# A two-layer mixer block on one core: an opening by quarters of the features instead of halves, and a retention that begins one step later in layer 0

## The chip, the cores and the metric

One Trainium2 chip, one of its cores. A core has a matrix engine (PE in the profile, with its weight loads as PEld), a vector engine (DVE), a scalar engine (ACT), GpSimd (POOL) and a queue engine (SP) that issues most transfers. The metric is the device time of one execution in microseconds (us); the kernel before takes 1234.97 us, the median of three runs (1234.73 to 1236.95).

## The reference

Two layers run over a latent stream `x` and a context stream `ctx`, each 256 tokens by 1024 features, in fp32. Cut to what the opening of the kernel computes and what uses it:

```python
for l in range(DEPTH):                                   # DEPTH = 2
    mod_l = silu(c) @ w_mod[l] + b_mod[l]                # 6 * 1024 values for the latent stream
    mod_c = silu(c_ctx) @ w_mod[l] + b_mod[l]            # the same for the context
    sh1, sc1, g1, sh2, sc2, g2 = split(mod_l, 6)         # csh1, csc1, ... from mod_c
    h_lat = rmsnorm(x, norm_g[l, 0]) * (1 + sc1) + sh1
    h_ctx = rmsnorm(ctx, norm_g[l, 0]) * (1 + csc1) + csh1
    p_lat, p_ctx = h_lat @ w_in[l], h_ctx @ w_in[l]      # 9 * 256 columns of q, k, v, ..., then 4 * 1024 of gates
    y_c, s_f, s_b = retention(rope_less(q_c), k_c, v_c)  # both directions, 4 heads of 64
    y_l, _, _ = retention(rope(q_l), rope(k_l), v_l, s_f, s_b)
    merged = sum(sigmoid(gates[i]) * (branch[i] @ w_branch[i]) for i in range(4))
    x = x + g1 * rmsnorm(merged @ w_o[l], norm_g[l, 1])  # branches: retention, conv, Fourier, pool
    x = x + g2 * rmsnorm(swiglu(rmsnorm(x) * (1 + sc2) + sh2), norm_g[l, 3])
    # ctx in the same way, in layer 0 alone
```

## The kernel before

The features are kept transposed: eight chunks of 128 features on the partitions, 512 columns (256 latent tokens, then 256 context tokens). Every fp32 product is made of three matmuls of rounded parts, high by high, high by low and low by high (`mm3`, L206 to L210). Weights come in blocks of 512 KB: `_load` (L95) issues the transfer on SP, `_split` makes the high part on ACT (L103) and the low part on DVE (L113), into a ring of four buffer pairs; raw blocks have two buffers for each tag. The program is one list of steps. A step names the blocks that it needs, and `pump` runs ahead of the steps with loads and splits as far as buffers are free; each engine then works its instructions in the order in which they were written. A DMA on SP that waits for its buffer or its semaphore therefore holds those behind it.

The opening is `begin` (L1313 on), with `clear`, `v_part` and `qk_part` (L1066 to L1100). It loads `x`, normalises it (`x_norm`: squares on ACT L423, a power on POOL L429, the scaling on DVE L1335) and turns it (`x_turn`, L1344). Meanwhile it makes the shift and scale of the modulation: the two conditioning vectors, padded to 32 columns (`cs`), are the stationary operand, and a block of `w_mod` is streamed against them (`mod_mm`, L263). The rows of the result are copied out by ACT (`modrows`, L1367), transposed (`modt`, L279), and added to their biases on DVE (L284 to L286). With them `modulate` makes a chunk of the hidden stream (`hf` L461 and L463, `h0hi` L467, `h0lo` L450). Then V, K and Q of both streams are accumulated in PSUM banks that stay occupied (`vps`, `kps`, `qps`). Those banks are first set to zero by matmuls with a zero operand (L1076, L1080), some of which only keep the engine busy (`WARM`).

It does this by halves of the features. Half 0 (chunks 0 to 3) needs eight blocks of `w_mod`; each block holds one chunk of contraction rows by the shift and scale columns of half of the features, in two matmuls of 512 columns. After them the V, K and Q parts of half 0 (12 matmuls each) alternate with the eight blocks of half 1, and then the parts of half 1 follow. 24 parts of 12 make 288 matmuls of 256 columns. After the last Q part the gate steps begin (`g_step`, `gps`, L208 to L210, 512 columns). The rotary step of K and Q (`rotate`, ACT L722 and L724, DVE L725 to L727) runs beside them, with one buffer (`roper`), and needs the `rope` table, which `fixed` loads on SP. From the first `g_step` a generator `both` advances the retention piece by piece, one at each step (its transposes `ktp` L760, its states `st` L776, its scores, its output `y` L813).

Of the kernel before, what the change touches and what calls it, by code (L numbers as in the profile page):

```python
# [33 lines left out]
MOD_ORDER = (0, 2, 1, 3)  # L34
# [4 lines left out]
WARM = (3,)  # L39
# [22 lines left out]
class Weights:  # L62
# [76 lines left out]

    def split_to(self, nth):  # L140
# [17 lines left out]
def kernel(ctx: ExitStack, tc: tile.TileContext, a: dict, out: bass.AP):  # L158
# [46 lines left out]

    def mm3(ps, st, mv, first, last):  # L206
# [38 lines left out]
    chan = load(cst, [P, DEPTH, 2, 4], a["chan"], "chan", nc.scalar)  # L245
    bsel = load(cst, [P, 2], a["c_bsel"], "bsel", nc.scalar)
    e12 = load(dec, [P, 2, 2 * PIECE], a["c_e12"], "e12", nc.scalar)
    kexp = load(dec, [P, 2, 2], a["c_kexp"], "kexp", nc.scalar)
# [8 lines left out]
    def mod_mm(k, half, raw):  # L257
        if "ps" not in mods:
            mods["ps"] = bank("m", "modps")
        ps = mods["ps"]  # L260
        for j in range(2):
            q = 2 * half + j
            nc.tensor.matmul(  # L263
                ps[32 * q : 32 * q + 32, :],
                lhsT=cs[:, k, :],
                rhs=raw[:, j * 512 : (j + 1) * 512],
                start=(k == 0),
                stop=(k == KC - 1),
            )
# [4 lines left out]
    def mod_cols(half, tiles, rows):  # L274

        pt = bank("b", f"modt{half}", [4, 64])
        hs = slice(64 * half, 64 * half + 64)
        for cb in range(4):
            nc.tensor.transpose(pt[:, cb, :], rows[hs, cb * P : (cb + 1) * P], ident[hs, hs])  # L279
        am, sh = tiles  # L280
        ks = slice(4 * half, 4 * half + 4)
        for s in range(2):
            b = [bcol[:, 0, kind, ks] for kind in range(2)]
            nc.vector.tensor_tensor(sh[:, s, ks], pt[:, :, s], b[0], op=ALU.add)  # L284
            nc.vector.tensor_tensor(am[:, s, ks], pt[:, :, 32 + s], b[1], op=ALU.add)
            nc.vector.scalar_tensor_tensor(  # L286
                am[:, s, ks], am[:, s, ks], 1.0, gcol[:, 0, 0, ks], op0=ALU.add, op1=ALU.mult
            )
# [325 lines left out]
    def mixer(l, h, hnext, start=None):  # L614
# [124 lines left out]
        def both():  # L739
            yield from retention(0)  # L740
# [320 lines left out]
        if l == 0:  # L1061
            vps, kps, qps = {}, {}, {}

            def clear():
# [4 lines left out]
                yield  # L1069
                for i in range(2):  # L1070
                    vps[i], kps[i] = bank("a", f"vps{i}", [2, MIX]), bank("a", f"kps{i}")
                for n in (0, *WARM):
                    for i in range(2):
                        for ps in (vps[i].rearrange("p a b -> p (a b)"), kps[i]):
                            for _ in range(n or 1):
                                nc.tensor.matmul(ps, lhsT=z[:, :P], rhs=z, start=n == 0, stop=False)  # L1076
                    yield
                for i in range(2):
                    qps[i] = bank("b", f"qps{i}", keep=True)
                    nc.tensor.matmul(qps[i], lhsT=z[:, :P], rhs=z, start=True, stop=False)  # L1080
                yield

            def v_part(w, half, t):
                ps, ts = vps[t // 2][:, t % 2, :], slice(t * P, (t + 1) * P)
                for i in range(4):
                    k, sl = 4 * half + i, slice(i * MIX, (i + 1) * MIX)
                    mm3(ps, (h[0][k][:, ts], h[1][k][:, ts]), (w.hi[:, sl], w.lo[:, sl]), False, k == KC - 1 and t % 2 == 1)
                if half and t % 2:
                    for j in range(2):
                        center(vps[t // 2][:, j, :], t - 1 + j)  # L1090

            def qk_part(w, half, isq, c, s):
# [499 lines left out]
```

## Time and profile before

| | us |
|---|---|
| median of three runs | 1234.97 (1234.73 to 1236.95) |
| the profiled execution | 1234.56 |
| its span, first to last instruction | 1232.8 |
| PE busy in it | 1196.1 (97%) |
| DVE, ACT, POOL busy | 783.7 (64%), 452.1 (37%), 41.1 (3%) |
| PE's first matmul starts | 9.13 |
| first V matmul starts | 25.84 |
| first gate matmul starts | 76.37 |

The span is about 1.8 us shorter than the execution's time, which also covers what lies around it; the profiled execution is 0.4 us below the median. A line of the profile names the line of the program, the engine, the operation, the tile written and the tiles read, with start and duration in us. Matmuls are pipelined: the distance of two starts tells what one costs in a row, and its own duration is longer. In square brackets stands how long the engine was idle before an instruction, and what ended that.

### The profile page before, as it was taken

How to read it: one execution, taken by the hardware profiler on the slowest of the kernel's cores; microseconds unless marked ns; L12 is line 12 of the kernel's file. 1: busy time of each engine (PE TensorE's matmuls, PEld its weight loads, DVE VectorE, ACT ScalarE, POOL GpSimd, SP SyncE). 2: the span in 40 equal slices, each digit the busy share in tenths (PEclk: the TensorE clock that was granted, in tenths of full speed). 3: DMA queues.
4: the chain of work that ended last, by engine and by line, in shares of the span. 5: the costliest groups of instructions: out<-in, count | busy, mean ns of one | idle time of the engine just before them, and what ended most of it. 6: DMA issues, size and time to landing. Idle time of an engine off the chain costs nothing.

```text
span 1232.8 us, 17240 instructions
## 1 busy us (share of the span) xinstructions
PE 1196.1 (97%) x6774; PEld 1025.4 (83%) x6774; DVE 783.7 (64%) x1274; ACT 452.1 (37%) x714; POOL 41.1 (3%) x39
## 2 busy tenths in 40 slices
PE   6999999999999989999999999989999999999997
PEld 3687878888888788888888888789889998999986
DVE  4455654477876565776777774476666666666644
ACT  4332332332232443222322222454345445444532
POOL 1500000000000000000000000000000000000000
PEclk9999999999999999999999999999999999999999
DMA  8543424456655234666766773334355563666672
GB/s 302 178 114 94 116 86 156 157 170 144 219 184 187 69 103 140 219 211 141 262 192 201 233 263 92 115 123 144 117 162 185 177 232 123 188 187 185 194 220 86
DMA packets 66435, 205.65 MB, mean 167 GB/s; under 512 B 14641, under 2 KB 18481, under 8 KB 66353
## 3 DMA queue, kind: packets, MB, share of 16 engines
q1 hardware_dynamic: 65200, 204.31, 53.1%
q8 instruction: 53, 0.87, 0.3%
q10 hardware_dynamic: 1152, 0.24, 0.1%
q14 instruction: 30, 0.24, 0.1%
HBM read 203.41 MB, written 1.11 MB: 166 GB/s over the span
## 4 chain that ended last, share of the span: by engine, by line
PE 89%; DVE 4%; ACT 3%; issue 1%; DMA 1%; POOL 0%; SPq 0%; DVEq 0%; POOLq 0%; ACTq 0%
PE up L210 10%; PE up L209 10%; PE up L208 10%; PE gate L208 7%; PE gate L210 7%; PE gate L209 7%; PE dn L210 4%; PE dn L209 4%; PE dn L208 4%; PE pb L208 2%; PE pb L210 2%; PE pb L209 2%; PE wo L210 1%; PE wo L208 1%; PE wo L209 1%
## 5 line engine op out<-in xcount | busy, mean ns | idle before, releaser
L318 DVE SCALAR_TENSOR_TENSOR mjunk<-raw_mod,crow 128x1024 bf16<-128x1024 f32 x128 | 156.4, 1222 | 8.7 <-DMA raw_mod<-in_w_modt 6.7
L209 PE MATMUL up<-hm0lo,hi_up 128*128 128x512 f32 (+1 forms) x384 | 143.3, 373 | 0.4 <-DVE hm0lo L450 0.4
L210 PE MATMUL up<-hm0hi,lo_up 128*128 128x512 f32 (+1 forms) x384 | 143.3, 373 | 0.1
L208 PE MATMUL up<-hm0hi,hi_up 128*128 128x512 f32 (+1 forms) x384 | 143.4, 373 | 0.0
L113 DVE TENSOR_TENSOR lo_up<-raw_up,hi_up 128x1024 fp32r<-128x1024 f32 x88 | 107.6, 1224 | 37.3 <-ACT hi_up L103 37.3
L113 DVE TENSOR_TENSOR lo_gt<-raw_gt,hi_gt 128x1280 fp32r<-128x1280 f32 x64 | 95.3, 1489 | 27.8 <-ACT hi_gt L103 27.5
L208 PE MATMUL gate<-h0hi,hi_gt 128*128 128x512 f32 x256 | 100.4, 392 | 0.0
L208 PE MATMUL up<-hm1hi,hi_up 128*128 128x256 f32 x352 | 99.8, 284 | 0.0
L209 PE MATMUL up<-hm1lo,hi_up 128*128 128x256 f32 x352 | 99.7, 283 | 0.1
L209 PE MATMUL gate<-h0lo,hi_gt 128*128 128x512 f32 x256 | 99.6, 389 | 0.0
L210 PE MATMUL up<-hm1hi,lo_up 128*128 128x256 f32 x352 | 99.6, 283 | 0.0
L210 PE MATMUL gate<-h0hi,lo_gt 128*128 128x512 f32 x256 | 99.6, 389 | 0.0
L103 ACT ACTIVATE hi_up<-raw_up 128x1024 fp32r<-128x1024 f32 x88 | 92.2, 1048 | 8.6 <-DMA raw_up<-in_w_up 8.0
L103 ACT ACTIVATE hi_gt<-raw_gt 128x1280 fp32r<-128x1280 f32 x64 | 81.0, 1266 | 24.9 <-DMA raw_gt<-in_w_gate 24.8
L113 DVE TENSOR_TENSOR lo_dn<-raw_dn,hi_dn 128x1024 fp32r<-128x1024 f32 x44 | 53.6, 1224 | 53.5 <-ACT hi_dn L103 53.5
L1013 ACT ACTIVATE sg<-gate 128x512 f32<-128x512 f32 (+1 forms) x64 | 31.3, 489 | 150.6 <-PE gate L210 150.6
L209 PEld LDWEIGHTS up<-hm0lo,hi_up 128*128 128x128 f32 x384 | 73.0, 190 | 13.1 <-DVE hm0lo L450 0.6
L210 PEld LDWEIGHTS up<-hm0hi,lo_up 128*128 128x128 f32 x384 | 72.9, 190 | 12.8 <-DVE lo_up L113 0.4
L208 PEld LDWEIGHTS up<-hm0hi,hi_up 128*128 128x128 f32 x384 | 72.9, 190 | 12.6
L103 ACT ACTIVATE hi_dn<-raw_dn 128x1024 fp32r<-128x1024 f32 x44 | 46.4, 1058 | 91.8 <-PE dn L210 65.1
L208 PE MATMUL gate<-hf0hi,hi_gt 128*128 128x256 f32 x256 | 73.3, 286 | 0.0
L210 PE MATMUL gate<-hf0hi,lo_gt 128*128 128x256 f32 x256 | 72.4, 283 | 0.0
(336 smaller groups left out, 2758.6 us busy)
## 6 DMA issues: line engine op xcount, KB each, us to landing
raw_up<-in_w_up SPq DMA_DIRECT2D x88, 512.0 KB, 3.9
raw_gt<-in_w_gate SPq DMA_DIRECT2D x64, 640.0 KB, 4.0
raw_mod<-in_w_modt SPq DMA_DIRECT2D x80, 512.0 KB, 3.8
raw_dn<-in_w_down SPq DMA_DIRECT2D x44, 512.0 KB, 4.3
raw_in<-in_w_in SPq DMA_DIRECT2D x28, 512.0 KB, 3.8
raw_mod<-in_w_mod SPq DMA_DIRECT2D x16, 512.0 KB, 4.5
raw_wo<-in_w_o SPq DMA_DIRECT2D x16, 512.0 KB, 4.0
grow<-gscr SPq DMA_DIRECT2D x6, 512.0 KB, 6.9
```

Of the source, the lines that this page charges most:

```text
L103: self.nc.scalar.activation(b.hi, b.raw, AF.Copy)
L113: self.nc.vector.tensor_tensor(b.lo, b.raw, b.hi.bitcast(F32), op=ALU.subtract)
L208: nc.tensor.matmul(ps, lhsT=st[0], rhs=mv[0], start=first, stop=False)
L209: nc.tensor.matmul(ps, lhsT=st[0], rhs=mv[1], start=False, stop=False)
L210: nc.tensor.matmul(ps, lhsT=st[1], rhs=mv[0], start=False, stop=last)
L318: nc.vector.scalar_tensor_tensor(junk, b.raw, 1.0, crow[s], op0=ALU.mult, op1=ALU.mult, accum_out=out()[:, s, i : i + 1])
L1013: nc.scalar.activation(sg, ps, AF.Sigmoid)
```

## The change

The opening takes the features by quarters, two chunks at a time. `w_mod` is laid out anew on the host: a block is now a quarter's 512 columns (shift and scale of 256 features) for two chunks of contraction rows, so a quarter needs four blocks. A block is eight matmuls of 128 columns, four of which write four groups of 32 partitions. The first four blocks go straight into the ring's high and low buffers. The blocks of quarter q + 1 stand in two pairs inside quarter q. A quarter has one transpose `modt` and three small DVE operations. The squares and the scaling of the odd row tiles go from ACT to DVE and those of the even ones to ACT; one of the four copies of the turned latents goes to ACT. The parts of V, K and Q are half as long and their matmuls are grouped by pass (high by high of all, then the mixed ones). The zero matmuls stand elsewhere: eight ahead of everything. Four small constant loads go from ACT's queue at the start to SP's in quarter 0. `both` gives one more turn away in layer 0 before the retention starts.

```diff
-WARM = (3,)
+WARM = (2, 0.5, 0, 1)
+    def mm3s(todo, last):
+        for n, (i, j) in enumerate(((0, 0), (0, 1), (1, 0))):
+            for m, (ps, st, mv) in enumerate(todo):
+                nc.tensor.matmul(ps, lhsT=st[i], rhs=mv[j], start=False, stop=last and n == 2 and m == len(todo) - 1)
...
-    e12 = load(dec, [P, 2, 2 * PIECE], a["c_e12"], "e12", nc.scalar)
+    def load_late():
+        for t, src in ((e12, "c_e12"), (kexp, "c_kexp"), (chan, "chan"), (bsel, "c_bsel")):
+            nc.sync.dma_start(t, a[src])
...
-    def mod_mm(k, half, raw):
+    def mod_mm(quarter, pair, raw):
-        ps = mods["ps"]
-        for j in range(2):
-            q = 2 * half + j
-            nc.tensor.matmul(
-                ps[32 * q : 32 * q + 32, :],
-                lhsT=cs[:, k, :],
-                rhs=raw[:, j * 512 : (j + 1) * 512],
+        ps = mods["ps"][:, quarter * P : (quarter + 1) * P]
+        for i in range(2):
+            k = 2 * pair + i
+            for q in range(4):
+                nc.tensor.matmul(
+                    ps[32 * q : 32 * q + 32, :],
+                    lhsT=cs[:, k, :],
+                    rhs=raw[:, (4 * i + q) * P : (4 * i + q + 1) * P],
...
         def both():
+            if l == 0:
+                yield
             yield from retention(0)
...
+        def x_sums(t):
+            for n in range(2):
+                if t % 2:
+                    nc.vector.scalar_tensor_tensor(
+                        junk, x, 1.0 / 1024.0, x, op0=ALU.mult, op1=ALU.mult, accum_out=ss[:, n : n + 1]
+                    )
+                else:
+                    square(xn[t][n], ss[:, n : n + 1])
+        def x_scale(t):
+            for n in range(2):
+                if t % 2:
+                    nc.vector.tensor_scalar(x, x, sc, None, op0=ALU.mult)
+                else:
+                    nc.scalar.activation(x, x, AF.Copy, scale=sc)
...
+        raw0 = [ring.tile([P, 1280], F32R, tag=("hi", "lo")[j % 2], name=f"mod0{j}")[:, :D].bitcast(F32) for j in range(4)]
+        steps.append(Step([], lambda: weights.fetch(1), tick=False, ahead=-1))
+        steps.append(Step([], loads, tick=False, ahead=-1))
+        first_step(0, opening, lambda: x_norm((0, 1)))
+        first_step(1, partial(lat_turn, "v"), partial(lat_turn, "a"))
+        first_step(2, partial(lat_turn, "v"))
+        split_of(vb[0])
+        first_step(3, opening)
+        add(lambda: cols(0), opening, lambda: hidden(0, 0))
+        V_(0, 0)
...
+        for q in range(4):
+            if q:
+                V_(q, 0)
+                add(lambda q=q: hidden(1, q))
+                for fn in (K_, Q_):
+                    for c in range(2):
+                        fn(q, c, 0)
+            if q == 3:
+                add(fixed)
+            for j in range(2):
+                if q < 3:
+                    mod_step(q + 1, j, *([more] if q < 2 else []))
+            V_(q, 1)
+            for j in range(2, 4):
+                if q < 3:
+                    mod_step(q + 1, j, *([more] if q == 0 and j == 2 else []))
+            K_(q, 0, 1)
+            if q < 3:
+                add(lambda q=q: (cols(q + 1), hidden(0, q + 1)))
```

On PE, from the last blocks of `w_mod` that the first projection needs (`modps` is the modulation's bank, `vps` a bank of V; zero matmuls left out), before:

```order
L263 MATMUL modps<-raw_mod_226,cs 32x512 x2
...
L263 MATMUL modps<-raw_mod_230,cs 32x512 x2
L263 MATMUL modps<-raw_mod_248,cs 32x512 x2
...
L263 MATMUL modps<-raw_mod_259,cs 32x512 x2
L279 MATMUL modt_320<-ident,modrows 128x64 x4
...
L208 MATMUL vps_295<-hi_v_317,h0hi_114 128x256
```

and now:

```order
L284 MATMUL modps<-mod_128,cs 32x128 x8
...
L284 MATMUL modps<-mod_129,cs 32x128 x8
...
L284 MATMUL modps<-mod_130,cs 32x128 x8
...
L284 MATMUL modps<-mod_131,cs 32x128 x8
...
L299 MATMUL modt_315<-ident,modrows 128x128
...
L1114 MATMUL vps_184<-hi_v_295,h0hi_110 128x256
```

Eight blocks of two matmuls stood ahead of the first projection, now four blocks of eight shorter ones.

On SP, the transfers behind the four loads of `x`, from the fourth block of `w_mod` on, before:

```order
L95 DMA raw_mod_199<-in_w_mod 128x1024
L95 DMA raw_mod_226<-in_w_mod 128x1024
L95 DMA raw_mod_230<-in_w_mod 128x1024
L95 DMA raw_mod_248<-in_w_mod 128x1024
L95 DMA raw_mod_259<-in_w_mod 128x1024
L95 DMA raw_v_277<-in_w_v 128x1024
L95 DMA raw_k_286<-in_w_k 128x1024
L1324 DMA x_303<-in_ctx 128x512
```

and now, from the third:

```order
L1458 DMA mod_130<-in_w_mod 128x1024
L94 DMA raw_v_208<-in_w_v 128x1024
L1458 DMA mod_131<-in_w_mod 128x1024
L1353 DMA x_211<-in_ctx 128x512
L1353 DMA x_212<-in_ctx 128x512
L1353 DMA x_215<-in_ctx 128x512
L1353 DMA x_216<-in_ctx 128x512
L94 DMA raw_k_219<-in_w_k 128x1024
L94 DMA raw_q_221<-in_w_q 128x1024
L94 DMA raw_mod_223<-in_w_mod 128x1024
```

The last block that the first projection needs was the eighth behind `x` and is now the fifth (three of `w_mod`, V's, the fourth of `w_mod`); the context's four halves and the first blocks of K and Q follow it.

On PE inside the stream of projections, the first block of `w_mod` that comes after the first projections and its neighbours (`kps`, `qps` are the banks of K and Q, `x0t` the turned inputs), before:

```order
L210 MATMUL kps_298<-h0hi_117,lo_k_389 128x256
L263 MATMUL modps<-raw_mod_311,cs 32x512 x2
L1080 LDWEIGHTS zero
L1080 MATMUL qps_446<-zero 128x512
L1080 LDWEIGHTS zero
L1080 MATMUL qps_448<-zero 128x512
L1344 MATMUL x0t_454<-ident,x_303 128x128
```

and now:

```order
L218 MATMUL qps_313<-h0hi_111,lo_q_392 128x256
L284 MATMUL modps<-raw_mod_223,cs 32x128 x8
L284 MATMUL modps<-raw_mod_299,cs 32x128 x8
L1114 MATMUL vps_186<-hi_v_295,h0hi_110 128x256
...
L1114 MATMUL vps_186<-lo_v_296,h0hi_111 128x256
L284 MATMUL modps<-raw_mod_377,cs 32x128 x8
L284 MATMUL modps<-raw_mod_395,cs 32x128 x8
L218 MATMUL kps_185<-h0hi_110,hi_k_369 128x256
```

Eight single blocks became six pairs, and the four blocks that are no longer in the stream are those ahead of the first projection. On SP the table of the rotary step (`rope`) now stands behind a third block of the input projection (`in014`), which waits for a ring buffer.

## Rows read from the trace of the kernel before

**Rows 1.** The page: the span.

```profile
span 1232.8 us, 17240 instructions
```

**Rows 2.** PE's waits from 0 to 120 us: in total, times, longest.

```profile
PE modps L263 <- DMA raw_mod<-in_w_mod: 9.6, 2, 9.1
PE x0t L1344 <- ACT hf L461: 1.6, 1, 1.6
PE vps L208 <- ACT h0hi L467: 1.2, 1, 1.2
```

**Rows 3.** Timeline of PE, 0 to 26 us: start, duration, instruction, idle before.

```profile
16.14 1.05 PE L263 MATMUL modps<-raw_mod,cs 128*32 128x512 f32 x4
...
21.29 1.05 PE L263 MATMUL modps<-raw_mod,cs 128*32 128x512 f32 x4
23.04 0.46 PE L279 MATMUL modt<-ident,modrows 64*128 64x64 f32 x4 [0.69 <-ACT modrows L1367]
...
25.84 0.47 PE L208 MATMUL vps<-hi_v,h0hi 128*128 128x256 f32 x1
```

**Rows 4.** Stretches: length, busy PE, PEld, DVE, ACT, POOL, clock, DMA share, GB/s.

```profile
0.00:5.00 5.00, 0.00 (x0) 0.00 (x0) 1.69 (x9) 1.50 (x2) 0.43 (x5) 1.00 0.58 172
5.00:10.00 5.00, 0.87 (x4) 0.22 (x4) 0.21 (x1) 2.68 (x7) 3.54 (x2) 1.00 0.88 298
10.00:15.00 5.00, 5.00 (x22) 1.52 (x20) 2.65 (x7) 0.21 (x2) 0.75 (x1) 1.00 0.91 312
15.00:20.00 5.00, 4.49 (x24) 1.27 (x20) 3.16 (x11) 0.00 (x0) 0.00 (x0) 1.00 0.95 350
```

**Rows 5.** Timelines of ACT and DVE, 0 to 30 us.

```profile
22.39 0.59 ACT L1367 ACTIVATE modrows<-modps 64x512 f32<-64x512 f32 x1 [12.18 <-PE modps L263]
...
24.00 0.60 ACT L461 ACTIVATE hf<-x0s,sh,am 128x256 f32<-128x256 f32 x1
...
26.75 1.04 ACT L103 ACTIVATE hi_k<-raw_k 128x1024 fp32r<-128x1024 f32 x1
...
27.82 1.22 DVE L113 TENSOR_TENSOR lo_k<-raw_k,hi_k 128x1024 fp32r<-128x1024 f32 x1 [0.40 <-ACT hi_k L103]
```

**Rows 6.** Timeline of PE around one block of `w_mod` in the stream.

```profile
40.96 0.28 PE L210 MATMUL vps<-hi_v,h0lo 128*128 128x256 f32 x1
41.17 1.05 PE L263 MATMUL modps<-raw_mod,cs 128*32 128x512 f32 x4
42.15 0.38 PE L208 MATMUL vps<-hi_v,h0hi 128*128 128x256 f32 x1
```

**Rows 7.** Timeline of PE: the eight state matmuls of the retention and the next.

```profile
87.61 0.66 PE L776 MATMUL st<-vd,kt 128*64 128x128 f32 x8
88.19 0.50 PE L208 MATMUL fu<-h0hi,hi_in 128*128 128x512 f32 x1
```

**Rows 8.** Timelines of PE, ACT and SP at the opening's end.

```profile
59.65 0.42 SPq L199 DMA_DIRECT2D rope<-in_c_rope  x1
...
76.37 0.40 PE L208 MATMUL gps<-h0hi,hi_in 128*128 128x512 f32 x1
...
78.87 0.38 ACT L724 ACTIVATE q<-qps 128x256 f32<-128x256 f32 x1
...
80.75 0.39 ACT L722 ACTIVATE roper<-qps 128x256 f32<-128x256 f32 x1 [1.50 <-DVE q L727]
```

**Rows 9.** Timeline of PE, 444 to 447 us.

```profile
444.24 0.42 PE L210 MATMUL up<-hm0hi,lo_up 128*128 128x256 f32 x1
444.45 0.41 PE L208 MATMUL up<-hm0hi,hi_up 128*128 128x256 f32 x1
...
446.26 0.28 PE L208 MATMUL up<-hm0hi,hi_up 128*128 128x256 f32 x1
446.38 0.28 PE L209 MATMUL up<-hm0lo,hi_up 128*128 128x256 f32 x1
```

**Rows 10.** Stretch of the matmuls of rows 9; columns as in rows 4.

```profile
443.60:446.80 3.20, 3.20 (x18) 3.20 (x19) 0.23 (x1) 0.72 (x2) 0.00 (x0) 0.61 0.73 230
```

More of the change, by code (lines that the diff above doesn't have):

```diff
@@ L33 @@
 NK = SEQ // 2 + 1
-MOD_ORDER = (0, 2, 1, 3)
 Q, K, V, G, BG, CG, XV, FU, PU, GATE = 0, 2, 4, 6, 8, 10, 12, 14, 16, 18
@@ L138, in pump, with fetch @@
             self.flush()
+    def fetch(self, n):
+        for _ in range(n):
+            assert self._load(self.first[0])
+            if self.first.pop(0).split:
+                self.loaded += 1
+            else:
+                self.read += 1
     def split_to(self, nth):
@@ L1078, in clear @@
[L1078 to L1088, printed above, removed]
+                ends = [x for i in range(2) for x in (vps[i].rearrange("p a b -> p (a b)"), kps[i])]
@@ new lines, in clear, with v_part @@
+                z_ = lambda ps, first: nc.tensor.matmul(ps, lhsT=z[:, :P], rhs=z, start=first, stop=False)
+                for n, rounds in enumerate(WARM):
+                    for i in range(int(4 * rounds)):
+                        z_(ends[i % 4], n == 0 and i < 4)
+                    if n == 2:
+                        for i in range(2):
+                            qps[i] = bank("b", f"qps{i}", keep=True)
+                            z_(qps[i], True)
+                    yield
+            def v_part(w, quarter, s):
+                todo = []
+                for t in (2 * s, 2 * s + 1):
+                    ps, ts = vps[s][:, t % 2, :], slice(t * P, (t + 1) * P)
+                    for k in (2 * quarter, 2 * quarter + 1):
+                        sl = slice(k % 4 * MIX, (k % 4 + 1) * MIX)
+                        todo.append((ps, (h[0][k][:, ts], h[1][k][:, ts]), (w.hi[:, sl], w.lo[:, sl])))
+                for n, (i, j) in enumerate(((0, 0), (1, 0), (0, 1))):
+                    for m, (ps, st, mv) in enumerate(todo):
+                        nc.tensor.matmul(ps, lhsT=st[i], rhs=mv[j], start=False, stop=quarter == 3 and n == 2 and m == 3)
+                if quarter == 3:
@@ L1313, in begin @@
     def begin(rt, ot, v_part, qk_part, fixed, clear):
-        xn, xt, ready, steps = {}, [], [], []
+        xn, xt, steps = {}, [], []
         tiles = mod_tiles(0, 0)
         decay = decays()
+        rows = {}
         def x_load(t, new):
@@ L1370, in add, with mod_part @@
+        def mod_part(quarter, pair, blk):
+            ps = mod_mm(quarter, pair, blk.raw)
+            if pair == 3:
+                rows[quarter] = md.tile([P, 512], F32, tag="rows", name="modrows")[:, :P]
+                nc.scalar.activation(rows[quarter], ps, AF.Copy)
         def add(*fns, blocks=(), free=None):
             steps.append(Step(list(blocks), lambda: [f() for f in fns], free=free, tick=False, ahead=0))
-        def mod_step(half, k, *fns):
-            b = Block(a["w_mod"][k, half], f"mod00{k}{half}", split=False)
-            add(partial(mod_first, half, k, b), *fns, blocks=[b])
@@ L1377, in part, with mod_step @@
-        def part(fn, half, b, free, *args):
-            add(partial(fn, b, half, *args), blocks=[b], free=[b] if free else [])
+        def mod_step(quarter, pair, *fns):
+            b = Block(a["w_mod"][quarter, pair], f"mod00{quarter}{pair}", split=False)
+            add(partial(mod_part, quarter, pair, b), *fns, blocks=[b])
         vb = [Block(a["w_v"][0, i], f"v0{i}") for i in range(2)]
@@ new lines, in begin, with __init__, first_step, first_load @@
+        cols = lambda q: mod_cols(q, tiles, rows[q])
+        raw0 = [ring.tile([P, 1280], F32R, tag=("hi", "lo")[j % 2], name=f"mod0{j}")[:, :D].bitcast(F32) for j in range(4)]
+        class First:
+            def __init__(self, j):
+                self.raw = raw0[j]
+        def first_step(j, *fns):
+            add(partial(mod_part, 0, j, First(j)), *fns)
+        def first_load(j):
+            nc.sync.dma_start(raw0[j], a["w_mod"][0, j])
+        def begin_loads():
+            for t in range(2):
+                x_load(t, partial(ot, [512]))
+            for j in range(3):
+                first_load(j)
```

214 lines of the change are left out of this document (87 added, 127 removed).

## The prediction

> **What bounds the kernel now.** I read the page first: PE is busy nearly the whole span of 1232.8 us [rows 1], so a change that shortens an idle stretch, or takes matmul time away, is worth what it takes away there. Second, PE's waits: in the first 120 us they come to 9.6 us for the first blocks of `w_mod` and two waits of 1.6 and 1.2 us for the hidden stream [rows 2]. Up to 120 us it has only one other, of 0.7. Third, the timeline of the first 26 us, which shows what the waits alone don't: most of what PE does before 25.84 us is modulation, turns and zero matmuls, and the first V matmul comes 4.55 us after the start of the eighth block's products at 21.29 [rows 3]. Fourth, the stretches: the DMA engines are 0.88 to 0.95 busy from 5 us on, at 298, 312 and 350 GB/s [rows 4]. So the start of the projections is set by the bytes ahead of the eighth block, and by a chain behind it: its products, the copy out by ACT, the transpose, the biases, `hf` at 24.00, the rounded parts [rows 3, 5]. From 25.84 to the first gate matmul at 76.37 [rows 8], 50.53 us, PE is the bound: 288 matmuls at a distance of 0.12 (40.96 to the next start without a block in between, and rows 9 at full clock) are 34.56 us, and the eight blocks of half 1 stand among them.
>
> **Landing of the blocks.** Before, the first projection needs 1.05 MB of `x` and eight blocks of 0.524, which is 5.24 MB. Now it needs `x` and five blocks (four of `w_mod`, one of V), 3.67 MB. Two bounds. By the stretches 0.86 MB have moved at 5 us, 2.35 at 10 and 3.91 at 15 [rows 4], so 3.67 MB are there at 14.2 at the earliest, if nothing behind the fifth block takes a share. Before, the products of the fifth block started at 16.14 [rows 3], with as many bytes ahead: that is the late end. I take 15.0: three small loads of some 0.08 MB are gone from ahead of it and the first four blocks no longer wait for a raw buffer, but later transfers share the engines.
>
> **From the last block to the first projection.** Before 4.55 us. Now: the block's 8 matmuls some 0.6 (below), a copy out of 128 columns instead of 512, 0.35 against 0.59 [rows 5], one transpose of 0.35 in place of four in 0.46 [rows 3], three small DVE operations instead of six, 0.3, `hf` 0.6 [rows 5] and the rounding of one chunk 0.4, with starts in between: 2.7. The four zero matmuls lie inside this. V's split is ahead of it. So the first projection starts at 15.0 + 2.7 = 17.7, with 16.9 and 19.0 as bounds, against 25.84. The normalisation of `x` must fit into the same time: it now ends a little past 10 us, since the squares are split over two engines, so the turns are ready before the third block is. **8.1 us** are gained here.
>
> **The stretch of the projections.** The 288 matmuls stay, 34.56. Eight blocks cost 42.15 - 41.08 = 1.07 each and about 0.1 for a slower matmul after them [rows 6]: 9.4 in all. Each now has 8 matmuls of 128 columns in two passes, 16 passes, and what they cost depends on how many column groups run together. The nearest row is the retention's state: eight records of 128 columns, in two column groups, take 0.58 to the next start [rows 7]. That is four steps of 0.109 and 0.15 of overhead, so two groups run together and a pass of 128 columns takes 0.109. If four groups run together, a pair of blocks is 8 steps, 0.87 + 0.15 + 0.12 = 1.15, and six pairs are **6.9**. If only two do, a pair is 16 steps, 2.0, and six are **12.1**. No row of this kernel shows four groups at once. I take four, because the block of before ran its two groups together in every one of 16 cases (1.07 for four passes of 512 columns, where one after the other they would take 1.7), and nothing in the rows ties that to two.
>
> [...]
>
> The rest of the stretch: five turns of 0.55 follow the first projection where it was four, one of the latents having moved behind it (2.75 against 2.2); three transposes of the modulation with their gap, 1.05 against 0.45; the two zeroings of Q, 0.5, are gone from here; slow first matmuls and switches 0.65 as before (what is left of 50.53). PE's waits were 2.8 [rows 2]. Now the blocks of K and Q are what comes late: K's has 5.24 MB to its end, as the eighth block had, so it lands at about 20.5, its high part takes 1.04 and its low part 1.22 [rows 5], so 22.8. The first V part ends at 19.3 and a turn at 19.8, so K waits 1.7 us and its low pass a few tenths. Q's block lands 1.5 us later and costs a few tenths more. With the context's squares, scalings and splits on the same two engines I put 2.8 on quarter 0 and 1.2 on the others, 4.0, bounds 2 and 6. The sum is 34.56 + 6.9 + 2.75 + 1.05 + 0.65 + 4.0 = 49.9 against 50.53, **0.6 us** better. The gates begin at 67.6 instead of 76.37.
>
> **The end of the opening.** Behind the last Q part the rotary step frees the banks of Q; it has one buffer, so the second bank of Q was begun at 80.75, 1.50 us after the first had been read at 79.25 (78.87 + 0.38) and the `rope` table had been issued at 59.65, 16.7 us ahead of the gates [rows 8]. Now `rope` stands on SP behind a third block of the input projection, which waits for a ring buffer, and should land 1 to 2 us after the first gate matmul; the first rotation, done early before, then waits for it. Both banks of K come first, each with a round of some 2.2 (0.66 of reading and the 1.5), so Q's first bank is free some 6.1 us after the start of the gates; the second gate step, which takes it, comes after some 5.6 (24 matmuls of 512 columns at a little under twice 0.12). I put 0.6 us on this, bounds 0 and 2. Behind it on SP are the tables of Fourier and pooling, the decay vector and its reading back; none is used in the first 15 us of the gates.
>
> **Edits at nothing.** The retention one step later moves a transpose and eight state matmuls (0.58, rows 7) past one gate projection; PE does as much in another order, and the branch is first used several steps later. What covers it is that PE has a queue of gate matmuls; without that it would cost one wait, under 1 us, and it could as well save one where the transposes now meet a K that is rotated late. The four small loads on SP cost issue time, some 0.4 each, in quarter 0, where SP is ahead. Grouping by pass lets the high pass start before the low part is there; it is inside the waits above.
>
> **Sum.** 1234.56 of the profiled execution - 8.1 - 0.6 + 0.6 = 1226.5. After the opening PE is the bound again, so what is gained at its end arrives at the end. The profiled execution lies 0.4 below the median, which is less than these terms can tell; I forecast **1226.5**, about 0.7% faster. Its own bounds: landing 0.8 earlier or 1.3 later, waits 2.0 either way, the end 0.6 less or 1.4 more, the retention 1 either way. All together are 1222.1 and 1232.2; most of the forecast's cases lie in 1223.5 to 1230.
>
> **Rivals.** *Two column groups at a time.* The blocks cost 12.1 instead of 6.9, so 1231.7. For it: every row shows two groups, none four. Against it: nothing in the rows needs to stop at two. Chance 0.14.
>
> *The opening becomes a chain of DVE, ACT and splits.* DVE was 3.1 of 5 us busy and ACT idle between 15 and 20 us [rows 4]; now the work that took from 5 to 45 us (two normalisations, three splits, two quarters) is pressed into 15 us less. If each quarter's hidden chunks come 1 us late and the rotary step loses its 2 us, 4 x 1 + 1.4 come off: 1231.9. Chance 0.09.
>
> *The first blocks do not land earlier,* because the engines share their time among all that is issued and the fifth block lands when the eighth did: the first 8.1 are cut to 2, and the rest stays: 1232.6. Against it: before, the fifth block's products started 5.15 us ahead of the eighth's [rows 3]. Chance 0.04.
>
> [...] Chance 0.04.
>
> [...]
>
> **How the numbers follow.** Forecast 0.69, rivals 0.14, 0.09, 0.04 and 0.04. What a measurement of this kernel tells from no change is about 0.2%, 2.5 us: faster means below 1232.5. The forecast, the two column groups and most of the chain are faster (0.69 + 0.14 + 0.08 = 0.91); the rest of the chain and the late landing are within 0.2% (0.05); the clock is slower (0.04). The range reaches over the forecast's bounds and the first two rivals, 1222.0 to 1232.0, and leaves out the last two and a few cases at its ends.
>
> **What would show it.** Right: the first V matmul between 16.9 and 19.0; pairs of modulation blocks 1.15 long, with four records starting together; K's first matmul waiting for its high part at about 20 us; the first gate matmul near 67.6; a short wait of the second gate step; the same distance from the first gate to the end as before. Wrong: pairs of 2 us, granted clock under 1 between 18 and 68 us, a first gate later than 72, or more PE waits after the gates than before.

## The result and the profile after

The changed kernel takes 1227.53 us (median of four runs, 1226.88 to 1227.95) against 1234.85 for the kernel before beside it; the ratio is 0.9938, with 0.9925 to 0.9951 as its 95% interval. 1226.5 had been forecast. The profiled execution takes 1227.5 with a span of 1225.7, some 7.0 shorter than before [rows 1].

PE's waits in the first 120 us, as in rows 2 (what is waited for, us in total, times, longest):

```profile
PE vps L1094 <- DVE zero L1090: 4.0, 1, 4.0
PE gps L222 <- ACT q L744: 2.5, 1, 2.5
PE modps L284 <- DMA mod<-in_w_mod: 2.2, 2, 1.2
PE kps L218 <- DVE lo_k L112: 0.9, 1, 0.9
PE vps L1114 <- ACT h0hi L487: 0.6, 1, 0.6
PE kps L218 <- ACT hi_k L102: 0.3, 1, 0.3
```

The first is only the time until the zero matmuls may begin. The 9.6 us for `w_mod` are 2.2, mostly because zero matmuls now stand in the time before the first block, which itself starts little earlier (8.75 against 9.13). New is the second: 2.5 us of the second gate step, behind the opening. Its timeline, with rows of PE from the fourth block on, as rows 3, 6 and 8 have them for the kernel before (start, duration, instruction, idle before):

```profile
13.89 0.64 PE L284 MATMUL modps<-mod,cs 128*32 128x128 f32 x16 [1.03 <-DMA mod<-in_w_mod]
...
14.94 0.33 PE L299 MATMUL modt<-ident,modrows 128*128 128x128 f32 x1
...
16.73 0.93 PE L1114 MATMUL vps<-hi_v,h0hi 128*128 128x256 f32 x4 [0.60 <-ACT h0hi L487]
...
24.33 1.08 PE L284 MATMUL modps<-raw_mod,cs 128*32 128x128 f32 x32
25.34 0.74 PE L1114 MATMUL vps<-hi_v,h0hi 128*128 128x256 f32 x4
...
63.61 0.40 PE L222 MATMUL gps<-h0hi,hi_in 128*128 128x512 f32 x1
...
68.85 0.39 PE L224 MATMUL gps<-h0hi,lo_in 128*128 128x512 f32 x1
71.72 0.50 PE L222 MATMUL gps<-h0hi,hi_in 128*128 128x512 f32 x1 [2.48 <-ACT q L744]
...
74.11 0.63 PE L224 MATMUL gps<-h0hi,lo_in 128*128 128x512 f32 x1
74.54 0.63 PE L222 MATMUL gps<-h0hi,hi_in 128*128 128x512 f32 x1
```

The first V matmul comes at 16.73 instead of 25.84 [rows 3], the first gate matmul at 63.61 instead of 76.37 [rows 8]: 9.1 and 12.8 us earlier, the second including the first. Of the 12.8 us only 7.0 reach the end of the span. 2.48 go in the wait that ends at 71.72; from 73.26 on, 1.5 us behind it, matmuls of 512 columns stand 0.43 apart instead of 0.23. The stretch there (columns as in rows 4) shows a granted clock of 0.50, where it is 1.00 from 63.6 to 68.8, while PE is busy all the time:

```profile
73.20:76.20 3.00, 3.00 (x8) 2.32 (x7) 2.54 (x5) 3.00 (x5) 0.00 (x0) 0.50 0.00 0
```

Seven distances stand at 0.43, which is another 1.5 us. The stretches of the start, to hold against rows 4:

```profile
5.00:10.00 5.00, 3.76 (x25) 1.08 (x22) 2.28 (x8) 1.83 (x4) 4.08 (x3) 1.00 1.02 365
10.00:15.00 5.00, 3.93 (x63) 2.58 (x64) 2.86 (x4) 2.13 (x4) 0.00 (x0) 1.00 1.03 409
```

Before, the same two moved 298 and 312 GB/s.

### The profile page after: what moved, and what is told of

It reads as the page before. It is cut to its first block, busy times and chain, and to the rows that moved or that the text cites. A ratio compares the mean times of both kernels' runs of the same rounds, so it can differ in the third digit from the quotient of the medians.

```text
span 1225.7 us, 17608 instructions
## 1 busy us (share of the span) xinstructions
PE 1190.2 (97%) x6959; PEld 1030.1 (84%) x6960; DVE 784.2 (64%) x1277; ACT 451.6 (37%) x713; POOL 40.7 (3%) x39
## 4 chain that ended last, share of the span: by engine, by line
PE 86%; DVE 5%; ACT 3%; DMA 2%; issue 2%; POOL 1%; SPq 0%; DVEq 0%; POOLq 0%; ACTq 0%
PE up L224 10%; PE up L223 10%; PE up L222 9%; PE gate L222 7%; PE gate L223 7%; PE gate L224 7%; PE dn L224 4%; PE dn L223 4%; PE dn L222 4%; PE pb L222 2%; PE pb L223 2%; PE pb L224 2%; PE wo L222 1%; PE wo L224 1%; PE wo L223 1%
```

## The experiments

Twelve kernels ran in three groups, each group with its own runs of the kernel before. Medians of different groups differ by that kernel's own drift (1235.55, 1236.82, 1235.82), so across groups the ratio counts. "Last block" is the start of the products of the last modulation block that the first projection needs; times in the last three columns are of each profiled execution.

| kernel | median us | ratio to before, interval | last block | first V | first gate |
|---|---|---|---|---|---|
| before | 1234.85 | 1 | 21.29 | 25.84 | 76.37 |
| after | 1227.53 | 0.9938 (0.9925 to 0.9951) | 13.89 | 16.73 | 63.61 |
| rope_early | 1224.01 | 0.9909 (0.9896 to 0.9922) | 14.84 | 18.10 | 64.92 |
| on_time | 1227.69 | 0.9937 (0.9925 to 0.9948) | 13.94 | 17.20 | 64.06 |
| two_groups | 1227.91 | 0.9938 (0.9926 to 0.9951) | 14.37 | 17.24 | 64.63 |
| consts_first | 1228.16 | 0.9945 (0.9933 to 0.9957) | 16.18 | 19.02 | 65.82 |
| rope_warm | 1223.41 | 0.9898 (0.9884 to 0.9911) | 14.24 | 17.07 | 64.26 |
| rope_cold | 1225.08 | 0.9912 (0.9899 to 0.9926) | 15.17 | 18.43 | 66.07 |
| k_first | 1228.37 | 0.9934 (0.9920 to 0.9947) | 15.55 | 18.38 | 65.22 |
| two_deep | 1232.32 | 0.9969 (0.9958 to 0.9980) | 15.94 | 19.20 | 71.17 |
| before_late | 1235.50 | 0.9997 (0.9988 to 1.0006) | 21.23 | 25.77 | 77.05 |
| tiny_first | 1229.64 | 0.9951 (0.9938 to 0.9964) | 16.55 | 19.38 | 66.20 |
| e_first | 1226.95 | 0.9933 (0.9920 to 0.9946) | 14.55 | 17.82 | 64.67 |
| rope_warm_bg | 1223.35 | 0.9901 (0.9887 to 0.9915) | 14.10 | 16.93 | 63.74 |

**The wait behind the opening.** On SP the rotary table stands behind a block of the input projection. In the changed kernel (SP's issue, then DVE's first use):

```profile
61.87 0.43 SPq L207 DMA_DIRECT2D rope<-in_c_rope  x1
...
67.06 0.69 DVE L746 TENSOR_TENSOR roper<-roper,rope 128x512 f32<-128x512 f32 x1 [3.64 <-DMA rope<-in_c_rope]
```

The edit of rope_early puts the load one quarter ahead:

```diff
-            if q == 3:
+            if q == 2:
                 add(fixed)
```

> The changed kernel with one edit: the loads of the rotary, Fourier and pooling tables stand on SP one quarter earlier, ahead of the first block of the input projection. Theory: the 2.48 us that the second gate step waits for Q's bank come from the rotary table landing at 67.06, 3.45 us after the first gate matmul, and the matmuls at the lower clock behind it (some 1.5 us) come from that wait; so the wait and the slow stretch both go, 1227.5 - 4.0 = 1223.5. Rival 1: the four rounds of the rotary step are themselves the limit, so the wait keeps 1.5 us or more and the time falls by under 1.5. Rival 2: the clock falls at that place anyway; the wait goes, 2.5 are gained, 1225.

Measured: 1224.01, ratio 0.9909, 3.5 us less than the changed kernel by the medians, with intervals that do not overlap. The table is issued at 47.48, PE's only waits up to 150 us are those of the start, and the stretch of the two gate steps is busy at the full clock:

```profile
47.48 0.42 SPq L207 DMA_DIRECT2D rope<-in_c_rope  x1
```

```profile
64.90:75.90 11.00, 11.00 (x51) 9.06 (x50) 9.58 (x18) 4.36 (x9) 0.00 (x0) 1.00 0.34 106
```

So the wait came from the table's late landing; the four rounds of the rotary step are fast enough, and the first rival falls. The low clock went with the wait, and the second falls with it. The low clock does not always follow the wait, though: eight kernels of the table have this wait (2.4 to 3.1 us: after, on_time, two_groups, consts_first, k_first, two_deep, tiny_first, e_first), and in e_first, behind 2.57 us of it, the matmuls of 512 columns stand 0.23 apart from 73.21 on. Without the wait the clock is 1.00 there in rope_early, as above, and in the kernel before (76 to 90 us).

**The retention one step later.** on_time takes the later start back:

```diff
         def both():
-            if l == 0:
-                yield
             yield from retention(0)
```

> The changed kernel without the later start of the retention in layer 0. Theory: PE does the same work in another order and the later start is worth nothing, within 0.5 us of 1227.5. Rival 1: the retention one step earlier puts its first transposes straight behind the wait for Q's bank, with K rotated late, so it waits and costs 1 us or more: 1228.5 to 1230. Rival 2: the later start has cost something by moving small matmuls next to others, and without it the time falls by 1 or more.

Measured: 1227.69 against 1227.53, and the ratios are 0.9937 and 0.9938. The waits of the opening are the same, the gate's among them (2.4). The later start is worth nothing that can be measured here.

**How many column groups run together.** two_groups changes only the order of the eight matmuls of a block:

```diff
-        for i in range(2):
-            for q in range(4):
+        for q0, i, q1 in [(q0, i, q1) for q0 in (0, 2) for i in range(2) for q1 in range(2)]:
+            for q in (q0 + q1,):
```

> The changed kernel with the eight matmuls of a modulation block in another order: two column groups for both chunks, then the other two, so that at most two groups run together. Theory: four groups at a time is what makes a pair of blocks 1.0 to 1.1 us long; now it is 1.9 to 2.0, six pairs cost 5.4 us more and the first gate comes at 69 instead of 63.61; 1227.5 + 5.4 = 1233. Rival: a block of short matmuls is limited by its 16 weight loads or by its issue and not by the column groups, and its length changes by under 0.2 us; 1227.5 to 1228.5.

Nothing changed (1227.91), but the row says that the edit had not done what it was for. A pair of blocks in two_groups:

```profile
24.85 1.10 PE L284 MATMUL modps<-raw_mod,cs 128*32 128x128 f32 x32
```

These are the 16 matmuls of two blocks, in two passes each; the row of the changed kernel reads 1.08. At 0.109 a pass [rows 7] they would take, by estimate, 3.5 one after the other and 1.74 two at a time, so here too four ran together: the later groups had simply started beside those ahead of them. The trace has the records of a pair four at a time in both kernels, within 21 ns in the changed kernel and 33 ns in two_groups. two_deep forces the matter by giving the eight matmuls only two groups:

```diff
-                    ps[32 * q : 32 * q + 32, :],
+                    ps[32 * (q % 2) : 32 * (q % 2) + 32, :],
```

> The changed kernel with all eight matmuls of a modulation block in two of the four column groups: the sums for two of the groups are added into those of the other two, and the rest of the bank is zero, so the modulation of layer 0's first norm holds other values; the amount of work is the same. In the run with another order of the matmuls four records still started within 30 ns, so this is what forces two at a time. Theory: a pair of blocks takes 2.0 us instead of 1.08, six pairs cost 5.2 to 5.5 more, the four first blocks another 1 to 2 where they do not wait, the first gate matmul comes near 70 instead of 64, and the time is 1232.5 to 1234. Rival: a pair is limited by its weight loads or issue, stays under 1.3, and the time stays within 1.5 of 1227.5.

```profile
26.81 1.94 PE L285 MATMUL modps<-raw_mod,cs 128*32 128x128 f32 x32
```

A pair takes 1.94, its records start two at a time every 0.109, the first gate comes at 71.17, and the kernel takes 1232.32 (0.9969). So four groups do run together in the changed kernel, and that is worth 0.86 for each of six pairs, 5.2 us of the stretch (51.97 against 46.88 from the first V to the first gate is 5.1). In the time two_deep loses 4.8 by the medians and 3.8 by the ratios, out of the 7.3 that the change gains. That is less than the 7.6 us by which its first gate is later, 2.5 of them ahead of the first V: from the first gate to the end its profiled run needs 1160.1 against 1162.1. The stretch at the lower clock would be 1.5 of the difference if two_deep has none, which is not shown.

**The first transfers.** consts_first gives the four small loads back to ACT's queue at the start:

```diff
-    e12 = dec.tile([P, 2, 2 * PIECE], F32, name="e12")
+    e12 = load(dec, [P, 2, 2 * PIECE], a["c_e12"], "e12", nc.scalar)
... (chan, bsel and kexp in the same way)
-                add(load_late)
```

> The changed kernel with the four small constant loads back on ACT's queue at the start. Theory: they are small (77 KB) but many packets and hold ACT's first square; the fourth block of the modulation lands some 0.5 us later than 13.85, the turns of the latents end near 13 instead of 12.8, and the first V matmul comes 0.5 us later, 1228.0. Rival 1: these loads are what kept the first transfers at 300 GB/s before; the fourth block lands at 15 or later and the first V matmul 1.2 us or more later, 1228.7 or more. Rival 2: no difference, 1227.5, since the queue was full before through waits for raw buffers only.

The rates fall nearly to those of the kernel before, 298 and 312 [rows 4]:

```profile
5.00:10.00 5.00, 3.35 (x23) 1.20 (x20) 1.74 (x6) 1.44 (x4) 3.64 (x3) 1.00 0.87 299
10.00:15.00 5.00, 4.46 (x54) 2.38 (x46) 2.07 (x4) 2.74 (x4) 0.50 (x1) 1.00 0.91 323
```

The fourth block starts at 16.18 and the first V matmul at 19.02, as the first rival said; the time rises by less (ratio 0.9945), which lies inside the intervals. tiny_first and e_first split the four: `chan`, `bsel` and `kexp` (11 KB) go back to ACT's queue, or `e12` alone (66 KB). What stays on SP, in tiny_first and then in e_first:

```diff
...
-        for t, src in ((e12, "c_e12"), (kexp, "c_kexp"), (chan, "chan"), (bsel, "c_bsel")):
+        for t, src in ((e12, "c_e12"),):
```

```diff
...
-        for t, src in ((e12, "c_e12"), (kexp, "c_kexp"), (chan, "chan"), (bsel, "c_bsel")):
+        for t, src in ((kexp, "c_kexp"), (chan, "chan"), (bsel, "c_bsel")):
```

> The changed kernel with three of the four constant loads back on ACT's queue at the start: 11 KB in rows of 64, 8 and 16 bytes. Theory: it is the number of small pieces that slows the transfers beside them, so the rate from 5 to 15 us falls to 300 to 340 GB/s and the first V matmul comes at 18.3 to 19.0. Rival: it is the 66 KB of the fourth load or their sum, and these three change under 0.5 us: first V matmul 16.7 to 18.1, 1227.5.

> The changed kernel with the fourth constant load alone (66 KB in rows of 528 bytes) back on ACT's queue at the start. Theory of the small pieces: one third of the pieces of all four, so a part of their effect, 360 to 390 GB/s from 10 to 15 us, the first V matmul within 0.5 us of 17.3. Rival: this load is the cause; the rates fall to 300 to 325 GB/s and the first V matmul comes at 18.5 to 19.

tiny_first, then e_first:

```profile
5.00:10.00 5.00, 2.67 (x15) 0.77 (x16) 1.65 (x6) 1.47 (x5) 3.72 (x3) 1.00 0.96 306
10.00:15.00 5.00, 4.92 (x60) 3.12 (x53) 1.57 (x3) 1.91 (x3) 0.45 (x1) 0.66 0.88 284
```

```profile
5.00:10.00 5.00, 3.83 (x24) 1.34 (x22) 2.45 (x8) 2.37 (x6) 4.17 (x3) 1.00 1.03 368
10.00:15.00 5.00, 5.00 (x62) 3.26 (x60) 1.12 (x3) 1.53 (x3) 0.00 (x0) 1.00 1.04 405
```

In the opening the three loads of 11 KB cost all of it, and the one of 66 KB nothing beyond what kernels with the same loads differ by (14.55 for the fourth block, against 13.89 to 14.84). In the time the two stand beside each other at 0.9951 and 0.9933, with intervals that overlap. The effect does not follow the small pieces as I had it: SP's issues show where the time goes. In the changed kernel the three blocks of `w_mod` and V's are issued one after the other; in tiny_first SP stands still between the blocks:

```profile
3.07 1.85 SPq L1458 DMA_DIRECT2D mod<-in_w_mod  x3
4.96 0.64 SPq L94 DMA_DIRECT2D raw_v<-in_w_v  x1
6.17 0.33 SPq L1458 DMA_DIRECT2D mod<-in_w_mod  x1
```

```profile
3.06 5.69 SPq L1458 DMA_DIRECT2D mod<-in_w_mod  x3
9.80 0.33 SPq L94 DMA_DIRECT2D raw_v<-in_w_v  x1
10.17 0.43 SPq L1458 DMA_DIRECT2D mod<-in_w_mod  x1
```

What ends SP's waits stands in the trace of the changed kernel: the fourth block of `w_mod` is issued at 6.17, after a wait of 0.6 for the third half of `x`, which lands at 6.16; the first half of the context at 7.30, after 0.8 for the last half of `x`, which lands at 7.29; Q's block at 11.29, after 0.6 for the third block of `w_mod`, which lands at 11.27. Counted in the order of issue over both queues, each of the three is the eighth load behind the one that it waits for. In tiny_first three more loads stand ahead, and the waits come earlier and are longer: the last half of `x` lands at 8.40 and SP issues the third block at 8.42 (4.49 in the changed kernel), the first block lands at 9.78 and V's is issued at 9.80 (4.96). So fewer transfers are under way. The rate falls behind that stand of SP; each number is the mean of half a us, from 0 to 20 us, first in the changed kernel and then in tiny_first:

```profile
GB/s 0 0 0 24 181 274 231 337 311 225 274 322 327 368 369 391 399 426 361 410 426 434 426 401 401 414 406 402 389 389 401 426 401 401 418 418 369 410 418 401
```

```profile
GB/s 0 0 0 27 178 240 356 373 262 193 235 311 308 344 340 380 386 372 185 198 188 377 246 254 279 295 246 303 315 332 352 348 340 373 414 422 426 430 401 418
```

From 9 to 10.5 us it is 185 to 198 in tiny_first and 361 to 426 in the changed kernel. The pieces of the small loads take little of the engines' time themselves. ACT's queue over the same 20 us (packets, MB, share of 16 engines), in the same order:

```profile
q10 hardware_dynamic: 576, 0.16, 3.3%
```

```profile
q10 hardware_dynamic: 1008, 0.17, 4.7%
```

The 1.4% more are 0.28 us of all engines, and the fourth block comes 2.7 us later. The kernel before stood in the same way: SP waited 4.0 us, until its first block had landed at 9.00, before it issued the third at 9.02. With one load more (e_first) SP issues V's block at 6.24 and the fourth at 7.04, instead of 4.96 and 6.17, and that costs nothing yet. So what costs here is the landing that each issue of SP waits for, which moves with the number of loads ahead (three or one), not with their bytes (11 or 66 KB); that the small pieces add nothing at all is not shown (the three loads have three times the pieces of the one).

before_late moves the four loads alone, in the kernel before:

```diff
...
         def ctx_load():
             x_load(2, lambda n: rt("am", [512], n, 3))
             x_load(3, lambda n: rt("ys", [512], n, 2))
+            for t, src in ((e12, "c_e12"), (kexp, "c_kexp"), (chan, "chan"), (bsel, "c_bsel")):
+                nc.sync.dma_start(t, a[src])
```

> The kernel before with one part of the change alone: its four small constant loads go from ACT's queue at the start to SP's, behind the context. Theory: these loads, 77 KB, hold the first transfers at 298 and 312 GB/s from 5 to 15 us; without them the rates are 350 to 410 as in the changed kernel, the eighth block of the modulation starts some 2.5 us earlier than 21.29, the first V matmul near 23.3, and the time is 1234.9 - 2.3 = 1232.5 or a little more. Rival: the old opening was slow because its blocks waited for raw buffers; the rates stay near 300, and the time stays within 0.7 of before.

Measured: 0.9997 (0.9988 to 1.0006), first V matmul at 25.77. The rate rises at first and then falls:

```profile
5.00:10.00 5.00, 1.10 (x4) 0.22 (x4) 1.74 (x6) 2.05 (x6) 4.21 (x3) 1.00 0.98 351
10.00:15.00 5.00, 5.00 (x17) 1.60 (x16) 0.41 (x2) 0.00 (x0) 0.00 (x0) 1.00 0.84 278
15.00:20.00 5.00, 5.00 (x28) 1.61 (x25) 3.30 (x8) 0.00 (x0) 0.00 (x0) 1.00 0.88 288
```

Four blocks are issued by 5.07, the next at 10.86, 12.56, 14.27 and 16.37: from the fifth on each waits for PE to be done with a buffer (in the kernel before six such waits of SP come to 6.8 us up to 20 us), and PE is busy throughout. So the old opening had two limits one behind the other, and in it the edit alone is worth nothing. A part of the second is the clock, by the times alone: the first three blocks take 5.34 us here, 4.48 in the kernel before and a later one 1.05 [rows 3]. What the edit would be worth there at the full clock was not tried.

k_first issues K's first block ahead of the fourth modulation block.

```diff
...
-        steps.append(Step([], lambda: weights.fetch(1), tick=False, ahead=-1))
+        steps.append(Step([], lambda: weights.fetch(2), tick=False, ahead=-1))
```

> The changed kernel with the first block of K issued ahead of the fourth block of the modulation instead of behind the context. Theory: the bytes ahead of the fourth block set the start, so it lands 0.524 MB later at some 400 GB/s, 1.3 us, and the first V matmul comes at 18.0 to 19.0 instead of 16.7 to 17.7; K's waits of 1.2 us for its parts go, so the first gate matmul moves by under 0.5 from 64.3 and the time stays within 0.7 of 1227.5. Rival: the chain of the normalisation and the turns sets the start, the first V matmul stays, and the first gate comes 1.2 us earlier; 1226.3.

The fourth block starts at 15.55 and the first V matmul at 18.38: the bytes ahead do set the start, by 1.2 to 1.7 us for 0.524 MB (against 14.37 in two_groups and 13.89 in the changed kernel, whose fourth blocks wait for their transfers as well). SP issues the block 1.55 us later too, but the rate stays (413 GB/s from 10 to 15 us), so the engines were not short of work, and the bytes decide rather than the later issue. The time (1228.37, 0.9934) does not show it. K's waits did not go, they are 0.9 for its low part and 0.3 for its high part as in the changed kernel. So they are not for K's transfer, which had landed by 14.21 here. ACT makes K's high part behind the context's squares, in the changed kernel:

```profile
17.63 0.63 ACT L443 ACTIVATE junk<-x 128x512 bf16<-128x512 f32 x1
18.16 0.19 ACT L443 ACTIVATION_READ_ACCUMULATOR junk<-x 128x1 f32 x1
18.26 1.04 ACT L102 ACTIVATE hi_k<-raw_k 128x1024 fp32r<-128x1024 f32 x1
```

**The clock of the first blocks.** With the same code up to there, the first two blocks take 0.64 each in the changed kernel and 1.08 in rope_early and on_time. rope_warm and rope_cold are rope_early with 16 and 4 zero matmuls ahead instead of 8:

```diff
-WARM = (2, 0.5, 0, 1)
+WARM = (4, 0.5, 0, 1)
```

> The kernel of rope_early with 16 zero matmuls ahead of the first block of the modulation instead of 8, so that PE is busy from 4.0 until the first block lands near 9. Theory: the clock of the first two blocks is what differs from run to run (16 records take 0.65 in one run and 1.08 in three others of the same code), and it is lost in the idle 0.9 to 1.7 us between the zeros and the first block; now all four blocks take 0.65, the first V matmul comes at 16.7 to 17.2 instead of 18.1, and the time is 0.5 to 1 below rope_early's 1224.0. Rival: the zeros are in the way of the first block and the first V matmul comes no earlier than 17.5; 1224.0 or more.

> The kernel of rope_early with 4 zero matmuls ahead of the first block instead of 8. Theory: PE stands idle for 3 us before the first block, the clock is at the low level for the first three blocks and the turns between them, and the first V matmul comes at 18.5 or later; 1224.5 to 1225.5. Rival: the first blocks wait for their transfers anyway, the fourth starts as it lands, and the first V matmul stays between 16.7 and 18.1; 1224.0.

The first block in the changed kernel, in rope_early, in rope_warm and in rope_cold (the second takes as long as the first in each):

```profile
8.75 0.64 PE L284 MATMUL modps<-mod,cs 128*32 128x128 f32 x16 [1.17 <-DMA mod<-in_w_mod]
```

```profile
9.24 1.08 PE L284 MATMUL modps<-mod,cs 128*32 128x128 f32 x16 [1.67 <-DMA mod<-in_w_mod]
```

```profile
9.76 0.64 PE L284 MATMUL modps<-mod,cs 128*32 128x128 f32 x16
```

```profile
8.91 1.08 PE L284 MATMUL modps<-mod,cs 128*32 128x128 f32 x16 [3.04 <-DMA mod<-in_w_mod]
```

That the 1.08 are the lower clock is read from the times alone: the clock column reads 1.00 from 5 to 10 us in all four. In rope_warm the zero matmuls ahead stand 0.43 apart up to 8.2 us and 0.22 from 8.6 on, without a pause between them.

The first V matmul comes at 17.07 and 18.43, the medians are 1223.41 and 1225.08. With PE busy up to it the first block takes 0.64, and its delay by half a us costs nothing, since the fourth still waits 0.54 for its transfer. Between rope_warm, 0.9898 (0.9884 to 0.9911), and rope_early, 0.9909 (0.9896 to 0.9922), the intervals overlap: the forecast 0.5 to 1 us is not shown in the time, only in the first V matmul. rope_warm and rope_warm_bg (below) are the fastest kernels here, and both beat both given ones.

**Biases and gains later too.** rope_warm_bg moves the next two loads of ACT's queue behind the fourth block, on top of rope_warm:

```diff
...
         def loads():
             first_load(3)
+            nc.sync.dma_start(bcol, a["b_col"])
+            nc.sync.dma_start(gcol, a["g_col"])
             ctx_load()
```

> The kernel of rope_warm with the two loads of biases and gains (80 KB in rows of 384 and 256 bytes) moved from ACT's queue to SP's, behind the fourth block of the modulation. Theory: the same slowing by small pieces is left in the first 10 us, so the rate from 5 to 10 us rises from 361 to 390 GB/s or more, the fourth block lands 0.3 to 0.8 us earlier than 14.24, and the time falls to 1222.8. Rival: what is left of the first 10 us is the start of the queue, nothing moves, 1223.4; or the biases come late for the small operations near 15.5 and the first V matmul comes later.

Measured: 1223.35, first V matmul at 16.93, 356 GB/s from 5 to 10 us. Nothing moved by more than the measurement tells. With two loads fewer ahead of it SP issues the fourth block 0.8 us earlier (5.19 against 5.99), and its products start 0.14 earlier.

## Why the prediction was right, and where its steps were off

The way in which the change gains was forecast rightly: fewer bytes ahead of the first projection, and blocks that run in four column groups. That the time came within 1.0 us is luck in part: landing and stretch came out 1.0 and 3.0 us better than forecast, the end of the opening and the way from there to the end 3.4 and 1.7 us worse. Of the signs that were named, the first V matmul (16.73, forecast 16.9 to 19.0), the first gate (63.61, near 67.6) and an equal distance from there to the end (1162.1 against 1156.4) did not come as said.

- **Landing and first projection**: 8.1 us forecast, 9.1 measured (the first V matmul is at 17.2 to 18.1 in rope_early, on_time and two_groups, a gain of 7.7 to 8.6, so 16.73 is a good run). The chain behind the fourth block is 2.84 against 2.7. The landing at 13.89 lies outside my bounds, 14.2 to 16.1: I bounded it by the rate of before, and did not see that the rate itself was held down by SP's waits (4.0 us up to 9.02, and 234, 70 and 186 GB/s from 9 to 10.5 us). From 10 to 15 us the changed kernel moved 409 GB/s where I had reckoned with 312.
- **The modulation in the stream**: six pairs at 1.15 forecast. A pair takes 1.01 from its start to the next matmul (24.33 to 25.34), and 0.1 or so behind it. Right, and two_deep shows why: in two groups a pair takes 1.94. Eight steps of 0.109 are 0.87 of the 1.01.
- **Waits in the stretch**: 4.0 forecast, 1.2 measured (0.3 and 0.9 for K), which is why the stretch from the first V to the first gate is 46.9 and not 49.9. This term was sized too large. I had put the waits down to K's transfer and to crowding on ACT and DVE; the transfer is in time (it lands at 17.8, where I had 20.5, at the higher rate), and later quarters have no wait worth a row.
- **The end of the opening**: 0.6 forecast, 2.48 and 1.5 at the lower clock measured. This term was sized too small. The place and the releaser (Q's bank, behind the rotary step, behind the table) were as forecast; the table was there 3.45 us after the first gate matmul where I had put 1 to 2, since it waits behind a block of 512 KB and the gates begin 4 us earlier than I thought. The stretch at a clock of 0.50 was not in the sum: I had weighed the clock for the opening itself, where it did not fall, and not behind the new wait.
- **To the end**: I had taken the rest for equal. rope_early has no wait there and still needs 1158.0 from first gate to end against 1156.4 before; rope_warm needs 1157.1. In the changed kernel some 1.7 us remain beside the wait and its clock. A wait of a down projection is 1.1 instead of 0.6; the end behind the last matmul is 0.4 longer; the rest I looked for in the stretches at the lower clock around 435 and 815 us, and did not settle: they read 0.50 for 3.4 us each, from 442.7, 821.6 and 831.8 before and from 435.0, 813.8 and 824.1 in the changed kernel, as many and as long.
- **The retention** was costed at nothing, and on_time shows that.
- **The rivals**: two column groups would have given 1231.7; two_deep, which is that case and also has its four first blocks in two groups, measured 1232.3 (1231.0 by its ratio). The chain of DVE, ACT and splits did not take hold. The slower case (0.04), the clock in the opening, did not come: in the changed kernel the first four blocks take 0.64 or 0.65 each, and the clock column reads 1.00 from 5 to 70 us. The 1.00 of the kernel before [rows 4] does not show a full clock in its opening: the first three blocks take 4.48 there, where a later one takes 1.05 [rows 3]. Their matmuls start, two at a time, 0.82 to 0.88 apart up to 12.54 and 0.47 behind it, so by the times the first two blocks ran at the lower level:

```profile
9.13 4.48 PE L263 MATMUL modps<-raw_mod,cs 128*32 128x512 f32 x12 [9.13 <-DMA raw_mod<-in_w_mod]
```

## What to carry to other kernels

When a stretch becomes shorter, look at every load that was issued inside it for the stretch behind it: a table whose load was issued 16.7 us ahead of the first gate matmul before was there 3.5 us behind it after, and one line gave half as much again as the whole change. Of an opening that waits for transfers, read first when its queue issues them and what each issue waits for; the bytes and the rates come after that. Matmuls that each fill a quarter of the columns took 1.08 us for a pair of blocks where their neighbours filled the other three quarters, and 1.94 where they filled one other; in the two orders tried (1.08 and 1.10) the order did not matter, but the places did.

## What the hardware showed that I had not expected

- Four column groups of 32 run together with matmuls of 128 columns, in either order of issue that was tried: 16 matmuls of two passes in 1.08 and 1.10 us, against 1.94 in two groups.
- Three loads of 11 KB together, ahead of the large ones, take the rate from 365 and 409 to 306 and 284 GB/s and delay the fourth block by 2 to 2.7 us, while SP waits for earlier loads to land: it issues the third block at 8.42 instead of 4.49. A load of 66 KB alone in their place leaves 368 and 405 GB/s.
- The first block's eight matmuls take 1.08 or 0.64 us from one kernel to the next with the same code ahead of them, when PE has stood idle 1.0 to 2.3 us before; with PE busy up to them they took 0.64 and 0.65 in the two kernels in which that was tried.
